# Head norms in phases, one row moved ahead on ScalarE, and first weights loaded by halves, in a fused four-branch encoder layer

## The chip, the cores and the metric

One Trainium2 chip, one of its cores. The metric is the device time of one execution in microseconds (us); lower is better.

## The reference

One layer of a bidirectional encoder over 2048 positions of width 1024, in float32. The input is RMS-normalised and projected once into 11 slots of 256 columns. Four mixers of 256 channels read these slots, each is multiplied by a SiLU gate, and one output projection of 1024 by 1024 adds the result to the input.

```python
def reference(x, mem, norm_g, w_in, w_out, ...):
    for l in range(DEPTH):
        h = rmsnorm(x, norm_g[l])
        proj = h @ w_in[l]
        a_u, a_v, a_g, b_q, b_k, b_v, b_g, c_in, c_g, d_q, d_g = jnp.split(proj, N_IN_SLOTS, axis=-1)
        y_a = chunked_spatial_gating(a_u, a_v, ...) * jax.nn.silu(a_g)
        y_b = neighbourhood_attention(b_q, b_k, b_v, ...) * jax.nn.silu(b_g)
        y_c = fourier_mixing(c_in, fn_w[l]) * jax.nn.silu(c_g)
        mem_n = rmsnorm(mem, mem_norm_g[l])
        y_d = memory_attention(d_q, mem_n, ...) * jax.nn.silu(d_g)
        x = x + jnp.concatenate([y_a, y_b, y_c, y_d], axis=-1) @ w_out[l]
```

Both attentions normalise each query and key head of 64 channels by its own RMS ("QK-norm"). That is the norm the change takes apart.

## The kernel before

**Precision and tiling.** Every operand of a large matmul is split into a high and a low part (`hi` rounded to fp32r, `lo` = raw - hi), and a product is three matmuls: hi*hi, hi*lo, lo*hi. x comes transposed, in tiles of 128 contraction rows by 512 positions (`get_x`, line 187; ScalarE makes hi on L137, VectorE makes lo on L138). Weights come two contraction steps at a time, 128 x 2 x 256, 256 KB (`get_w`, line 201): one DMA on L207, hi on ScalarE (L217), lo on GpSimd, or on VectorE for the second of two interleaved slots (`alt`) (L219). x, weights and `w_out` share five `raw` landing buffers.

**Order.** TensorE's order is written out by hand: `drive` (line 163) runs a filler (the projections) and spawned tasks (norms, transposes, attention, Fourier), and a task gives TensorE back by `yield d`, which makes it due again after d us of TensorE work. All other queues (ScalarE, VectorE, GpSimd, SP) are ordered by a list scheduler at build time: program order, moved up by `hp(offset)`. Each queue then runs strictly in its order.

**The sequence.** The sequence positions are in two halves, h = 0 and 1. For h = 0: `c_in` and `d_q` interleaved, one contraction step at a time, four groups of each (`proj`, `slot`); after 48 of these 64 groups `stats` (line 281) loads x in natural layout for the RMS (16 loads into five `nat` buffers, squares on L291, `rstd` by GpSimd on L294/L125). Then `pair_vv`, `a_u`, `pair_qk`, `a_g`, `d_g`, `b_g`, `c_g`; the same slots for h = 1; the output projection last (`out_proj`). Beside `pair_vv` run the memory keys and values (`mem_kv`, line 467; its squares are L495, each behind a load of `mem` on L494 into a `nat` buffer), the transposes of the queries (`emit_T` on L151 and L534/L535) and `bcast` (line 297).

**Norms of queries and keys.** `do_dq` (line 421) and `do_bqk` (line 431) take four PSUM banks. For each bank in turn `evac_nat` copies it to a `nat` tile scaled by `rstd` (L368, L370), and `head_norm` (line 373) squares it on ScalarE (L376), sums the heads on VectorE (L378), takes the power -1/2 on GpSimd (L124, L125) and scales in place on VectorE (L381). The task then yields 6.5 us (14 for the first `d_q`) and transposes.

**The row of norms.** `bcast` transposes `rstd` on TensorE into a PSUM tile, ScalarE copies the 8 x 128 row out (L302, at no raised priority), and two DMAs spread it over all partitions (L304, L306).

**Pipelined attention.** `pipeline` (line 546) runs scores two units ahead of transposes: while the first two score units go out, it yields `d[0]` after each (1.2 us for the memory attention, 0.3 for the other). Its two calls are the memory attention of h = 0, and everything that is left of both attentions.

Of the kernel before, what the change touches and what calls it, by code (L numbers as in the profile page):

```python
# [9 lines left out]
F32 = mybir.dt.float32  # L10
F32R = mybir.dt.float32r
AF = mybir.ActivationFunctionType
ALU = mybir.AluOpType
# [34 lines left out]
class Kern:  # L48
# [151 lines left out]

    def get_w(self, name, k, c0, alt):
        nc = self.nc
        with self.hp(8000 if k or alt else 15000 if self.wseen else 80000):
            raw = self.raw.tile([128, 2, 256], F32, name="raw")
            begin = not self.wseen and not alt
            self.wseen = True
            (nc.scalar if begin else nc.sync).dma_start(out=raw, in_=self.ins[name][k * 128:(k + 2) * 128, c0:c0 + 256].rearrange(  # L207
                "(t p) c -> p t c", t=2))
            if alt:
                w = self.att.tile([128, 2, 2, 256], F32R, name="PT", bufs=2)  # L210
                w = [w[:, 0], w[:, 1]]
            else:
                w = [self.wp.tile([128, 2, 256], F32R, name="hilo") for _ in range(2)]
            if begin:
                nc.vector.tensor_copy(out=w[0], in_=raw)
            else:
                nc.scalar.copy(out=w[0], in_=raw)  # L217
            eng = nc.vector if alt else nc.gpsimd
            eng.tensor_tensor(out=w[1], in0=raw, in1=w[0].bitcast(F32), op=ALU.subtract)  # L219
        return w  # L220

    def get_w2(self, k, ia, ib):
# [25 lines left out]
    def slot(self, h, c0, natural, ps, kstep):  # L248
        alt = bool(ps)
        if not ps:  # L250
            ps.extend(self.ps_acc.tile([128, 512], F32, name="acc") for _ in range(4))
        for k0 in range(0, 8, kstep):
            ks = range(k0, k0 + kstep)
            Xs = [self.get_x(h, k) for k in ks]
            if k0 % 2 == 0:
                wp = self.get_w("w_in", k0, c0, alt)
            for b in range(4):
                for k in ks:
                    X = Xs[k - k0]
                    wh, wl = wp[0][:, k % 2], wp[1][:, k % 2]  # L260
                    st, sp = k == 0, k == 7
                    if natural:
                        for t in (2 * b, 2 * b + 1):
                            o = ps[b][:, (t % 2) * 256:(t % 2) * 256 + 256]
                            xh, xl = X[t // 4]
                            sl = slice((t % 4) * 128, (t % 4) * 128 + 128)
                            first = st and t % 2 == 0
                            last = sp and t % 2 == 1
                            self.mm(o, xh[:, sl], wh, first, False, skip_group_check=True)
                            self.mm(o, xh[:, sl], wl, False, False, skip_group_check=True)  # L270
                            self.mm(o, xl[:, sl], wh, False, last, skip_group_check=True)
                    else:
                        cj, t = b // 2, b % 2
                        sl = slice(cj * 128, cj * 128 + 128)
                        xh, xl = X[t]
                        self.mm(ps[b], wh[:, sl], xh, st, False)
                        self.mm(ps[b], wh[:, sl], xl, False, False)
                        self.mm(ps[b], wl[:, sl], xh, False, sp)
                    yield
# [17 lines left out]
    def bcast(self, h):  # L297
        nc = self.nc
        ps = self.ps_mi.tile([8, 128], F32, name=self.nmi)
        self.tr(ps, self.rstd[h])  # L300
        row = self.sqp.tile([8, 128], F32, name="sa_o")
        nc.scalar.activation(out=row, in_=ps, func=AF.Copy, scale=0.5)  # L302
        d = self.d([8, 128], f"rs{h}")
        nc.sync.dma_start(out=d, in_=row)  # L304
        bc = self.const.tile([128, HS], F32, name="rbc")
        nc.sync.dma_start(out=bc, in_=d.rearrange("t p -> (t p)").unsqueeze(0).broadcast_to([128, HS]))  # L306
        self.rbc[h] = bc
        if h == 0:
            for cj in range(2):
                nc.gpsimd.tensor_tensor(out=self.cin[cj][:, 0:HS], in0=self.cin[cj][:, 0:HS], in1=bc, op=ALU.mult)  # L310
        yield
# [61 lines left out]
    def head_norm(self, q):  # L373
        nc = self.nc
        sq = self.sqp.tile([128, 512], F32, name="sq")
        nc.scalar.activation(out=sq, in_=q, func=AF.Square)  # L376
        ss = self.small.tile([128, 8], F32, name="hss")
        nc.vector.tensor_reduce(out=ss, in_=sq.rearrange("p (g d) -> p g d", d=HD), axis=AX.X, op=ALU.add)  # L378
        self.rsqrt(ss, ss, 1.0 / HD, 8)
        qv = q.rearrange("p (g d) -> p g d", d=HD)  # L380
        nc.vector.tensor_tensor(out=qv, in0=qv, in1=ss.unsqueeze(2).broadcast_to([128, 8, HD]), op=ALU.mult)  # L381
        return q
# [37 lines left out]

    def do_dq(self, h, ps):
        with self.hp(8000):
            qs = [self.head_norm(self.evac_nat(h, [(ps[b][:, j * 256:(j + 1) * 256], 2 * b + j) for j in range(2)]))
                  for b in range(4)]
        yield 6.5 if h else 14.0
        for b in range(4):
            self.emit_T("d", h * 4 + b, [qs[b][:, 0:256], qs[b][:, 256:512]])
            yield 3.3
        self.done.add(f"d_q{h}")

    def do_bqk(self, h, u, ps):
        with self.hp(8000):
            qs = [self.head_norm(self.evac_nat(h, [(ps[t], u * 4 + t)])) for t in range(4)]
        yield 6.5
        for b in range(2):
            for i, kind in ((1, "k"), (0, "q")):
                self.emit_T(kind, h * 4 + u * 2 + b, [qs[2 * b + j][:, i * 256:(i + 1) * 256] for j in range(2)])
                yield 3.3
        if u:
            self.done.add(f"b_qk{h}")  # L440
# [26 lines left out]
    def mem_kv(self):  # L467
        nc, I = self.nc, self.ins
        ps = [self.ps_sc.tile([128, 512], F32, name=self.nsc) for _ in range(2)]
        for k in range(8):  # L470
            with self.hp(0):
                raw = self.att.tile([128, 256], F32, name="dq", bufs=2)
                nc.sync.dma_start(out=raw, in_=I["memT"][k * 128:(k + 1) * 128, :])
                if k % 2 == 0:
# [6 lines left out]
                                               in1=m[:, 0].bitcast(F32), op0=ALU.mult, op1=ALU.subtract)  # L481
                if k % 2 == 0:
                    wt = self.att.tile([128, 2, 2, 512], F32R, name="PT", bufs=2)
                w = [wt[:, k % 2, 0], wt[:, k % 2, 1]]
# [5 lines left out]
        ss = self.c([128, 2, 2], "mss")  # L490
        for t in range(2):
            for u in range(2):
                raw = self.nat.tile([128, 512], F32, name="nat")
# [5 lines left out]
        q = self.nat.tile([128, 512], F32, name="nat")  # L499
# [8 lines left out]
            nc.vector.tensor_tensor(out=self.vm[:, t, :, HD:2 * HD], in0=v4,  # L508
                                    in1=self.vm[:, t, :, 0:HD].bitcast(F32), op=ALU.subtract)
        self.psum(True)  # L510
        self.head_norm(q)
        twice = self.att.tile([128, 512, 2], F32, name="PT", bufs=2)
        nc.vector.tensor_copy(out=twice, in_=q.unsqueeze(2).broadcast_to([128, 512, 2]))
        self.spawn(self.mem_k(twice), 20.0)
# [31 lines left out]
    def pipeline(self, items, d):  # L546
        A = 2
        units, n = [], 0
        last = {}
        it = iter(items)  # L550
        more = True
        while more or n < len(units) + A + 1:
            if n >= len(units) and more:
                try:
                    us, pv = next(it)
                    units.extend(us)
                    last[len(units) - 1] = pv
                except StopIteration:
                    more = False
            if n < len(units):  # L560
                units[n][0]()
                yield d[0]
            if 0 <= n - A < len(units):
                units[n - A][1]()
                yield d[1]
            if n - A - 1 in last:
                last.pop(n - A - 1)()
                yield d[2]
            n += 1
# [566 lines left out]
    def run(self):  # L1136
        tc = self.tc
        self.X, self.rstd, self.rbc = {}, {}, {}
        self.wseen = False
        self.t, self.seq, self.tasks, self.done = 0.0, 0, [], set()  # L1140
        self.scratch()
        self.constants()
        with tc.manual_schedule(engines={mybir.EngineType.PE}):
            with ExitStack() as es:
                P = lambda name, bufs, st=es: st.enter_context(tc.tile_pool(name=name, bufs=bufs, side="right",
                                                                            reuse_waits="tile"))
                self.nat = P("nat", 5)
                self.sqp = P("sqp", 2)
                self.att = P("att", 2)
                self.psum(False)  # L1150
                self.drive(self.main(P, es))
                self.pst.close()
# [98 lines left out]
```

## Time and profile before

| | |
|---|---|
| median of 3 runs | 872.2 us (871.57 to 875.5) |
| the profiled execution | 872.36 us, of which 870.6 is the span from its first to its last instruction |
| TensorE matmuls (PE) | 852.1 us busy, 98% of the span, 4448 matmuls |
| TensorE weight loads (PEld) | 82% |
| VectorE (DVE), ScalarE (ACT), GpSimd (POOL) | 58%, 47%, 38% |
| DMA | 177.9 MB, 204 GB/s on average |

A busy PE is matmuls in flight, so the 2% that is not busy is time in which TensorE waited for someone. "Granted clock" is the share of 2.4 GHz that the throttle gave; 0.5 is 1.2 GHz.

### The profile page before, as it was taken

Reading aid. Unit: us, or ns where it says so; the run is one execution under the profiler, and the core shown is the slowest. Engines: PE = TensorE matmul, PEld = TensorE weight load, DVE = VectorE, ACT = ScalarE, POOL = GpSimd, SP = SyncE. Lnnn points to the kernel's source line nnn. Section 1 sums busy time; section 2 is a strip of 40 time slices with the busy share of each in tenths; the row PEclk is TensorE's granted clock in tenths of the full one; section 3 lists DMA queues with packets and bytes.
Section 4 is the critical chain, followed back from the end, with each engine's and each line's share of the span. In section 5 each row is a group of like instructions: output and inputs, shape, how many; then the busy total and the mean of one; then the engine's idle time right before and its main releaser. Section 6 shows DMA issues by size and latency. Waiting matters only on the chain.

```text
span 870.6 us, 13653 instructions
## 1 busy us (share of the span) xinstructions
PE 852.1 (98%) x4448; PEld 713.6 (82%) x4448; DVE 502.6 (58%) x1064; ACT 407.1 (47%) x930; POOL 327.2 (38%) x368
## 2 busy tenths in 40 slices
PE   8999999999999999999999999999999999999998
PEld 7987788888788878887789888888878788888886
DVE  5356565587532557775454866676788777851111
ACT  5674353466632533544324655666765455521110
POOL 1136331155232122552232734434554433235550
PEclk9999999999999999999999999999999999999999
DMA  8967653346762562569669897864598987556661
GB/s 274 323 202 231 191 141 109 117 118 176 227 192 96 187 215 84 142 169 278 210 194 306 265 299 246 263 213 142 175 311 280 320 243 221 174 168 195 205 204 68
DMA packets 147463, 177.88 MB, mean 204 GB/s; under 512 B 29232, under 2 KB 105152, under 8 KB 147392
## 3 DMA queue, kind: packets, MB, share of 16 engines
q1 hardware_dynamic: 145104, 170.33, 62.6%
q0 software_dynamic: 1728, 6.29, 2.5%
q8 instruction: 35, 0.57, 0.3%
q10 hardware_dynamic: 560, 0.40, 0.2%
q14 instruction: 36, 0.29, 0.1%
HBM read 132.92 MB, written 44.05 MB: 203 GB/s over the span
## 4 chain that ended last, share of the span: by engine, by line
PE 78%; DMA 9%; DVE 6%; ACT 3%; issue 2%; POOL 2%; SPq 0%; ACTq 0%; DVEq 0%; POOLq 0%
PE acc L147 60%; PE w L147 8%; PE w L151 4%; PE sc L147 3%; DMA bt<-in_bias 2%; PE mi L147 2%; DMA nat<-in_mem 1%; DMA QD<-st 1%; DMA raw<-in_w_out 1%; DVE PT L535 1%; POOL hss L125 1%; DVE P L916 1%; DMA raw<-in_w_in 1%; DVE hilo L990 1%; DMA nat<-in_x 0%
## 5 line engine op out<-in xcount | busy, mean ns | idle before, releaser
L147 PE MATMUL acc<-hilo 128*128 128x512 f32 (+1 forms) x2880 | 710.5, 390 | 7.6 <-DVE nat L460 1.9
L147 PEld LDWEIGHTS acc<-hilo 128*128 128x128 f32 x2880 | 510.0, 189 | 100.1 <-issue 2.9
L219 POOL TENSOR_TENSOR hilo<-raw,hilo 128x512 fp32r<-128x512 f32 x52 | 68.5, 1319 | 171.2 <-ACT hilo L217 141.5
L231 POOL TENSOR_TENSOR hilo<-raw,hilo 128x512 fp32r<-128x512 f32 x32 | 43.3, 1352 | 114.4 <-ACT hilo L229 93.8
L983 POOL TENSOR_TENSOR nat<-nat 128x256 f32<-128x256 f32 x48 | 36.7, 764 | 93.4 <-DMA nat<-O 61.9
L229 ACT CAST hilo<-raw 128x512 fp32r<-128x512 f32 x64 | 39.7, 621 | 65.9 <-PE acc L147 54.9
L918 ACT ACTIVATE P<-P,smx 128x288 f32<-128x288 f32 (+1 forms) x64 | 39.9, 623 | 54.1 <-DVE smx L916 54.0
L535 DVE TENSOR_TENSOR PT<-w,PT 128x512 fp32r<-128x512 f32 (+2 forms) x96 | 61.2, 637 | 5.6 <-ACT PT L534 5.6
L1027 DVE TENSOR_TENSOR st<-acc,st 128x512 f32<-128x512 f32 (+1 forms) x33 | 21.6, 671 | 70.2 <-PE acc L147 69.9
L989 ACT CAST hilo<-nat 128x256 fp32r<-128x256 f32 x64 | 25.7, 406 | 76.3 <-PE acc L147 57.2
L534 ACT CAST PT<-w 128x512 fp32r<-128x512 f32 (+2 forms) x96 | 52.1, 543 | 18.6 <-PE w L151 18.0
L151 PE MATMUL w<-ident,P 128*128 128x128 f32 (+1 forms) x352 | 54.2, 273 | 1.0 <-DVE smx L916 1.0
L151 PEld LDWEIGHTS w<-ident,P 128*128 128x128 f32 (+1 forms) x352 | 43.0, 135 | 14.6 <-DVE smx L916 1.9
L217 ACT CAST hilo<-raw 128x512 fp32r<-128x512 f32 x51 | 31.3, 618 | 47.9 <-PE acc L147 35.4
L125 POOL TENSOR_TENSOR hss<-hss,mhalf 128x8 f32<-128x8 f32 x25 | 42.7, 1712 | 1.5
L916 DVE CUSTOM_DVE_ANT_0 P<-w,bt 128x288 f32<-128x288 f32 (+1 forms) x64 | 35.6, 556 | 13.2 <-DMA bt<-in_bias 10.3
L231 DVE TENSOR_TENSOR hilo<-raw,hilo 128x512 fp32r<-128x512 f32 x32 | 22.0, 689 | 31.0 <-ACT hilo L229 25.5
L607 ACT ACTIVATE P<-w,smx 128x256 f32<-128x256 f32 x64 | 29.7, 469 | 20.5 <-DVE smx L603 20.2
L958 POOL TENSOR_TENSOR ob<-tmp 64x128 f32<-64x128 f32 x64 | 30.1, 489 | 21.8 <-DVE tmp L954 20.6
L345 DVE TENSOR_TENSOR st<-acc,rbc 128x512 f32<-128x512 f32 x32 | 22.0, 686 | 26.4 <-PE acc L147 23.5
L138 DVE SCALAR_TENSOR_TENSOR hilo<-raw,gcol,hilo 128x512 fp32r<-128x512 f32 x32 | 26.2, 829 | 17.5 <-ACT hilo L137 16.6
L921 DVE TENSOR_SCALAR P<-P,smx 128x288 f32<-128x288 f32 (+1 forms) x64 | 34.0, 531 | 1.8
(170 smaller groups left out, 1062.7 us busy)
## 6 DMA issues: line engine op xcount, KB each, us to landing
raw<-in_w_in SPq DMA_DIRECT2D x119, 256.0 KB, 3.1
raw<-in_xT SPq DMA_DIRECT2D x32, 256.0 KB, 3.8
nat<-in_x SPq DMA_DIRECT2D x32, 256.0 KB, 5.3
G<-st SPq DMA_DIRECT2D x32, 256.0 KB, 3.4
nat<-G SPq DMA_DIRECT2D x64, 128.0 KB, 2.8
st<-in_x SPq DMA_DIRECT2D x32, 256.0 KB, 4.9
out_y<-st SPq DMA_DIRECT2D x31, 256.0 KB, 3.3
tab<-in_dft_s POOLq DMA_DIRECT2D x12, 512.0 KB, 5.2
```

Of the source, the lines that this page charges most:

```text
L125: nc.gpsimd.tensor_tensor(out=out, in0=out, in1=self.mhalf[:, :n], op=ALU.pow)
L147: self.nc.tensor.matmul(out=out, lhsT=lhsT, rhs=rhs, start=start, stop=stop, **k)
L151: self.nc.tensor.transpose(out=out, in_=in_, identity=self.ident)
L219: eng.tensor_tensor(out=w[1], in0=raw, in1=w[0].bitcast(F32), op=ALU.subtract)
L229: nc.scalar.copy(out=w[0], in_=raw)
L231: eng.tensor_tensor(out=w[1], in0=raw, in1=w[0].bitcast(F32), op=ALU.subtract)
L534: self.nc.scalar.copy(out=hi, in_=src)
L535: (eng or self.nc.vector).tensor_tensor(out=lo, in0=src, in1=hi.bitcast(F32), op=ALU.subtract)
L916: nc.vector.tensor_tensor_reduce(out=P[:, :n], in0=sc[:, :n], in1=bt[:, :n], op0=ALU.add, op1=ALU.min, scale=-1.0, scalar=3e38, accum_out= ...
L918: nc.scalar.activation(out=P[:, :n], in_=P[:, :n], func=AF.Exp, bias=sm[:, 1:2], scale=-1.0, accum_out=sm[:, 2:3])
L921: nc.vector.tensor_scalar(out=P[:, :n], in0=P[:, :n], scalar1=sm[:, 3:4], scalar2=None, op0=ALU.mult)
L983: mul.tensor_tensor(out=g, in0=o, in1=g, op=ALU.mult)
```

## The change

- `get_w`: the first load of each of the first two slots (`c_in` and `d_q`, k = 0) fetches only its first contraction step (128 KB), on ScalarE's DMA queue, with the highest priority; its hi and lo are made for that half alone (`c_in`: VectorE and GpSimd; `d_q`: ScalarE and VectorE). The other half is loaded on SP's queue when the slot reaches k = 1, and split by GpSimd (`c_in`) or VectorE (`d_q`) with a copy and a subtraction. First weights of later slots lose their offset of 15000 and get 8000 like all others.
- `bcast`: L302 gets the offset 9000.
- `head_norm` stops before the scaling, which becomes `scale_norm`. `do_dq` and `do_bqk` evacuate all four banks, take all four norms, yield 2.5 us, scale all four, and yield 4.5 us (12 for the first `d_q`).
- `pipeline`: 1.5 us more yield after each of the first two score units.

```diff
@@ -200,23 +200,34 @@
 
     def get_w(self, name, k, c0, alt):
         nc = self.nc
-        with self.hp(8000 if k or alt else 15000 if self.wseen else 80000):
+        with self.hp(8000 if k or self.wseen > 1 else 80000):
             raw = self.raw.tile([128, 2, 256], F32, name="raw")
-            begin = not self.wseen and not alt
-            self.wseen = True
-            (nc.scalar if begin else nc.sync).dma_start(out=raw, in_=self.ins[name][k * 128:(k + 2) * 128, c0:c0 + 256].rearrange(
-                "(t p) c -> p t c", t=2))
+            begin = k == 0 and self.wseen < 2
+            self.wseen += 1
+            src = self.ins[name][k * 128:(k + 2) * 128, c0:c0 + 256].rearrange("(t p) c -> p t c", t=2)
+            if begin:
+                nc.scalar.dma_start(out=raw[:, 0], in_=src[:, 0])
+            else:
+                nc.sync.dma_start(out=raw, in_=src)
             if alt:
                 w = self.att.tile([128, 2, 2, 256], F32R, name="PT", bufs=2)
                 w = [w[:, 0], w[:, 1]]
             else:
                 w = [self.wp.tile([128, 2, 256], F32R, name="hilo") for _ in range(2)]
+            eng = nc.vector if alt else nc.gpsimd
             if begin:
-                nc.vector.tensor_copy(out=w[0], in_=raw)
+                (nc.scalar.copy if alt else nc.vector.tensor_copy)(out=w[0][:, 0], in_=raw[:, 0])
+                eng.tensor_tensor(out=w[1][:, 0], in0=raw[:, 0], in1=w[0][:, 0].bitcast(F32), op=ALU.subtract)
             else:
                 nc.scalar.copy(out=w[0], in_=raw)
-            eng = nc.vector if alt else nc.gpsimd
-            eng.tensor_tensor(out=w[1], in0=raw, in1=w[0].bitcast(F32), op=ALU.subtract)
+                eng.tensor_tensor(out=w[1], in0=raw, in1=w[0].bitcast(F32), op=ALU.subtract)
+        if begin:
+            def rest():
+                with self.hp(8000):
+                    nc.sync.dma_start(out=raw[:, 1], in_=src[:, 1])
+                    eng.tensor_copy(out=w[0][:, 1], in_=raw[:, 1])
+                    eng.tensor_tensor(out=w[1][:, 1], in0=raw[:, 1], in1=w[0][:, 1].bitcast(F32), op=ALU.subtract)
+            self.rest[alt] = rest
         return w
 
     def get_w2(self, k, ia, ib):
@@ -254,6 +265,8 @@
             Xs = [self.get_x(h, k) for k in ks]
             if k0 % 2 == 0:
                 wp = self.get_w("w_in", k0, c0, alt)
+            elif k0 == 1 and alt in self.rest:
+                self.rest.pop(alt)()
             for b in range(4):
                 for k in ks:
                     X = Xs[k - k0]
@@ -299,7 +312,8 @@
         ps = self.ps_mi.tile([8, 128], F32, name=self.nmi)
         self.tr(ps, self.rstd[h])
         row = self.sqp.tile([8, 128], F32, name="sa_o")
-        nc.scalar.activation(out=row, in_=ps, func=AF.Copy, scale=0.5)
+        with self.hp(9000):
+            nc.scalar.activation(out=row, in_=ps, func=AF.Copy, scale=0.5)
         d = self.d([8, 128], f"rs{h}")
         nc.sync.dma_start(out=d, in_=row)
         bc = self.const.tile([128, HS], F32, name="rbc")
@@ -377,6 +391,10 @@
         ss = self.small.tile([128, 8], F32, name="hss")
         nc.vector.tensor_reduce(out=ss, in_=sq.rearrange("p (g d) -> p g d", d=HD), axis=AX.X, op=ALU.add)
         self.rsqrt(ss, ss, 1.0 / HD, 8)
+        return ss
+
+    def scale_norm(self, q, ss):
+        nc = self.nc
         qv = q.rearrange("p (g d) -> p g d", d=HD)
         nc.vector.tensor_tensor(out=qv, in0=qv, in1=ss.unsqueeze(2).broadcast_to([128, 8, HD]), op=ALU.mult)
         return q
@@ -420,9 +438,14 @@
 
     def do_dq(self, h, ps):
         with self.hp(8000):
-            qs = [self.head_norm(self.evac_nat(h, [(ps[b][:, j * 256:(j + 1) * 256], 2 * b + j) for j in range(2)]))
+            qs = [self.evac_nat(h, [(ps[b][:, j * 256:(j + 1) * 256], 2 * b + j) for j in range(2)])
                   for b in range(4)]
-        yield 6.5 if h else 14.0
+            ss = [self.head_norm(q) for q in qs]
+        yield 2.5
+        with self.hp(8000):
+            for q, s in zip(qs, ss):
+                self.scale_norm(q, s)
+        yield 4.5 if h else 12.0
         for b in range(4):
             self.emit_T("d", h * 4 + b, [qs[b][:, 0:256], qs[b][:, 256:512]])
             yield 3.3
@@ -430,8 +453,13 @@
 
     def do_bqk(self, h, u, ps):
         with self.hp(8000):
-            qs = [self.head_norm(self.evac_nat(h, [(ps[t], u * 4 + t)])) for t in range(4)]
-        yield 6.5
+            qs = [self.evac_nat(h, [(ps[t], u * 4 + t)]) for t in range(4)]
+            ss = [self.head_norm(q) for q in qs]
+        yield 2.5
+        with self.hp(8000):
+            for q, s in zip(qs, ss):
+                self.scale_norm(q, s)
+        yield 4.5
         for b in range(2):
             for i, kind in ((1, "k"), (0, "q")):
                 self.emit_T(kind, h * 4 + u * 2 + b, [qs[2 * b + j][:, i * 256:(i + 1) * 256] for j in range(2)])
@@ -508,7 +536,7 @@
             nc.vector.tensor_tensor(out=self.vm[:, t, :, HD:2 * HD], in0=v4,
                                     in1=self.vm[:, t, :, 0:HD].bitcast(F32), op=ALU.subtract)
         self.psum(True)
-        self.head_norm(q)
+        self.scale_norm(q, self.head_norm(q))
         twice = self.att.tile([128, 512, 2], F32, name="PT", bufs=2)
         nc.vector.tensor_copy(out=twice, in_=q.unsqueeze(2).broadcast_to([128, 512, 2]))
         self.spawn(self.mem_k(twice), 20.0)
@@ -559,7 +587,7 @@
                     more = False
             if n < len(units):
                 units[n][0]()
-                yield d[0]
+                yield d[0] + (1.5 if n < A else 0)
             if 0 <= n - A < len(units):
                 units[n - A][1]()
                 yield d[1]
@@ -1136,7 +1164,7 @@
     def run(self):
         tc = self.tc
         self.X, self.rstd, self.rbc = {}, {}, {}
-        self.wseen = False
+        self.wseen, self.rest = 0, {}
         self.t, self.seq, self.tasks, self.done = 0.0, 0, [], set()
         self.scratch()
         self.constants()
```

## Rows read from the trace of the kernel before

**Rows 1.** The page, part 1: busy time of TensorE and its share of the span.

```profile
PE 852.1 (98%) x4448; PEld 713.6 (82%) x4448; DVE 502.6 (58%) x1064; ACT 407.1 (47%) x930; POOL 327.2 (38%) x368
```

**Rows 2.** Busy time by stretch: us, then each engine (instructions), granted clock, DMA share, GB/s.

```profile
5.00:8.41 3.41, 1.10 (x6) 0.46 (x5) 2.76 (x4) 2.06 (x3) 1.71 (x1) 1.00 0.80 253
8.41:11.83 3.42, 3.42 (x13) 3.00 (x14) 2.74 (x8) 1.67 (x3) 0.00 (x0) 0.50 0.87 271
...
72.95:75.13 2.18, 0.40 (x2) 0.00 (x0) 0.85 (x2) 1.93 (x6) 0.83 (x2) 1.00 0.86 254
...
93.75:97.16 3.41, 1.69 (x7) 0.94 (x6) 2.42 (x5) 1.36 (x3) 1.87 (x2) 1.00 0.64 182
97.16:100.57 3.41, 3.41 (x9) 2.65 (x9) 2.43 (x7) 0.62 (x1) 1.80 (x3) 0.50 0.60 160
100.57:768.00 667.43, 660.14 (x3522) 552.65 (x3522) 431.89 (x938) 335.69 (x776) 248.42 (x272) 1.00 0.66 203
```

**Rows 3.** Timeline 0 to 9 us: start, duration, instruction, [idle before <- releaser].

```profile
0.72 0.40 ACTq L94 DMA_DIRECT2D gcol<-in_gcol  x1
...
1.16 0.48 ACTq L207 DMA_DIRECT2D raw<-in_w_in  x1
...
4.13 0.72 ACT L137 ACTIVATE hilo<-raw,gcol 128x512 fp32r<-128x512 f32 x1 [0.97 <-DMA gcol<-in_gcol]
...
6.03 0.43 DVE L215 CAST hilo<-raw 128x512 fp32r<-128x512 f32 x1 [0.39 <-DMA raw<-in_w_in]
...
6.54 1.71 POOL L219 TENSOR_TENSOR hilo<-raw,hilo 128x512 fp32r<-128x512 f32 x1 [5.24 <-DVE hilo L215]
...
8.30 0.71 PE L147 MATMUL acc<-hilo 128*128 128x512 f32 x1 [1.00 <-POOL hilo L219]
```

**Rows 4.** DMA queues, 3.4 to 4.5 us: ScalarE's queue (q10), packets, MB, share.

```profile
q10 hardware_dynamic: 105, 0.11, 41.5%
```

**Rows 5.** The page, costliest groups: busy us, mean ns of one, idle before.

```profile
L219 POOL TENSOR_TENSOR hilo<-raw,hilo 128x512 fp32r<-128x512 f32 x52 | 68.5, 1319 | 171.2 <-ACT hilo L217 141.5
...
L983 POOL TENSOR_TENSOR nat<-nat 128x256 f32<-128x256 f32 x48 | 36.7, 764 | 93.4 <-DMA nat<-O 61.9
...
L217 ACT CAST hilo<-raw 128x512 fp32r<-128x512 f32 x51 | 31.3, 618 | 47.9 <-PE acc L147 35.4
```

**Rows 6.** Timeline 46 to 76 us: TensorE's transposes that restart after the wait.

```profile
75.13 0.66 PE L151 MATMUL mi<-ident,nat 128*128 128x128 f32 x4 [1.78 <-ACT sa_o L302]
```

**Rows 7.** Timeline 46 to 76 us: the end of ScalarE's queue before that row.

```profile
73.20 0.63 ACT L495 ACTIVATE nat<-nat 128x512 f32<-128x512 f32 x1 [1.99 <-DMA nat<-in_mem]
...
73.83 0.56 ACT L534 CAST st<-mi 128x512 fp32r<-128x512 f32 x1
...
74.30 0.62 ACT L229 CAST hilo<-raw 128x512 fp32r<-128x512 f32 x1
...
74.82 0.26 ACT L302 ACTIVATE sa_o<-mi 8x128 f32<-8x128 f32 x1
```

**Rows 8.** The same timeline: the last load and the last square of the statistics.

```profile
47.89 0.33 SPq L290 DMA_DIRECT2D nat<-in_x  x1
...
52.76 0.59 ACT L324 COPY cin<-acc 128x512 f32<-128x512 f32 x1 [0.83 <-PE acc L147]
...
53.25 0.63 ACT L291 ACTIVATE nat<-nat 128x512 f32<-128x512 f32 x1
...
54.00 0.33 SPq L494 DMA_DIRECT2D nat<-in_mem  x1
```

**Rows 9.** The page, DMA issues: count, KB each, median us from issue to landing.

```profile
raw<-in_xT SPq DMA_DIRECT2D x32, 256.0 KB, 3.8
nat<-in_x SPq DMA_DIRECT2D x32, 256.0 KB, 5.3
```

**Rows 10.** Timeline 211 to 223 us: second norm of the tightest batch, its first transposes.

```profile
214.31 1.77 DVE L381 TENSOR_TENSOR nat<-nat,hss 128x512 f32<-128x512 f32 x1 [0.20 <-POOL hss L125]
...
218.08 0.60 PE L151 MATMUL w<-ident,nat 128*128 128x128 f32 x4
```

**Rows 11.** Line 219 as a source: who waited for it (us, times).

```profile
  PE acc L147: 1.0, 1
```

## The prediction

> **What bounds the kernel now.** I read the page first: TensorE is busy 852.1 of 870.6 us [rows 1], so a change off TensorE can only give back some of the 18.5 us in which it waits, and what it loses to a lower clock. Then the busy time by stretch [rows 2]. From 100.57 to 768 us TensorE is idle 7.3 us in all, in many small waits. The costly places lie early, and this change aims at two of them. At the start, TensorE works 1.10 us of the 3.41 before 8.41 us, and the next 3.42 us run at a granted clock of 0.50, which is 1.2 GHz: 13 matmuls that would take half of that at 2.4 GHz, so 1.71 us are lost. At 72.95 us it stands nearly still until 75.13. (A third place, 93.75 to 97.16 and 3.41 us of half clock behind it, isn't touched.) After that I took the timeline of the two places and followed each wait back.
>
> At the start [rows 3] the third matmul waits until 8.30 us for GpSimd's low part of the first weights, which took 1.71 us after VectorE's cast at 6.03, which waited for the 256 KB of weights. At 72.95 the transposes of the second query block restart at 75.13, released by L302 [rows 6]. But ScalarE's queue shows what L302 itself stood behind [rows 7]: a square of `mem` (L495) that waited 1.99 us for its load, then the evacuation L534 of the first block (priority 8000), then a weight cast L229 (8000), then L302 at 74.82.
>
> **The change part by part.** The sum is made against the profiled execution, 872.36 us (span 870.6 and 1.8 around it); the median of 872.2 is 0.16 below it.
>
> First weights by halves. In 3.4 to 4.5 us ScalarE's DMA queue, which then carries little but these weights, moved 0.11 MB [rows 4]; a half is 0.13 MB, so it is in at about 4.7, and I estimate 5.0 with its signal, against 6.03. The bounds: not before 4.13, where `gcol`, ahead in the same queue, released ScalarE; not after 5.5, which is 128 KB less at the 253 GB/s of that stretch [rows 2, 3]. The half cast takes about 0.25 (half of 0.43), GpSimd's subtraction on 128x256 takes 0.76 (the same shape on L983 [rows 5]), so the low part stands at 6.05 and the third matmul starts at 6.1 instead of 8.30. `d_q`'s half is second in the same queue and lands where the whole first load landed, at 6.0; copied by ScalarE (0.31, half of L217) and subtracted it is ready near 6.8. For that and for the second x tile I allow 0.9 us of waits. The 13 matmuls then take 1.71 us at full clock, so by 6.1 + 1.71 + 0.9 = 8.7 TensorE has done what it had done at 11.83: **3.1 us earlier**, 1.4 from the loads and 1.7 from the clock. Bounds: 0.9 (landing at 5.5, clock low as before) to 3.9 (landing at 4.3, no waits).
>
> The Trainium skill ("DMA: Bandwidth & Descriptors", "Issuing engines are not separate DMA queues") says that transfers issued by different engines interleave on the same 16 engines and that a second issuing engine saves only issue time. By it the half gains by its bytes alone, the start would give 2.6 instead of 3.1, and rival 1 below 867.8. The trace agrees that the engines are shared: this queue had 41.5% of their time in that stretch [rows 4], and the 3.1 goes by what it moved.
>
> The second halves. Two more loads on SP and, on GpSimd, a copy and a subtraction of 128x256. The trace has no GpSimd copy; it lies between nothing and the 0.76 of a subtraction with one input more, and I take 0.76, since it is the same shape and engine. The 1.5 us lie in GpSimd's idle time (5.24 us idle before its first subtraction [rows 3]), and are due when k = 1 begins, after the 36 matmuls of k = 0: at 1.71/13 = 0.13 each some 4.7 us behind 6.1. So they cost nothing; uncovered they would cost 1.5 once. VectorE's half of `d_q` is the same with 0.7.
>
> The row ahead on ScalarE. Offset 9000 lets L302 pass what is ready at the same time. L534 belongs to transposes that TensorE does before the row's own, and it already has 8000; yet it came out behind L495, which has no offset. So when the queue was laid out L495 was placed before L534 was ready, and L302, ready later still, can't pass L495 by priority. What it surely passes is L229: 74.30 instead of 74.82, **0.5 us**.
>
> So the gate stays, and the earlier start meets it. L495's load comes from a chain: the last square of the statistics (53.25, behind a copy L324 that waits for TensorE) frees the `nat` buffer in which the first `mem` load goes out at 54.00 [rows 8], and four loads and squares follow one another through it. The copy moves forward with TensorE, but the square needs its load, issued at 47.89. With the median of such loads, 5.3, it lands at 53.2 and the chain doesn't move; with the 3.8 of equal loads of `xT` it lands at 51.7 and the chain moves 1.5 [rows 9]. No row says which, so I take **1.0**, between the two, and keep 0 to 1.5. The row's time is then 75.13 - 0.5 - 1.0 = 73.6.
>
> Norms in phases. No operation is added; the scaling is emitted 2.5 us of TensorE work later and the transposes 0.5 later. The 0.5 us of projection matmuls thus comes ahead of the gate: **0.5** more is done when it opens. For the other batches I cost it at nothing: in the tightest one the second scaling ends at 216.1 and its transposes start at 218.1 [rows 10], 2.0 us of cover, 2.5 with the later yield. If the scaling slid by the full 2.5 us there, the wait would be about zero; by a further GpSimd power, some 2 us in one batch.
>
> Later first weights (8000 instead of 15000) and 1.5 us more yield after the first two score units of two pipelines: nothing. After the start no matmul waits for GpSimd's low weights (one wait of 1.0 us, the one above) [rows 11], ScalarE's cast L217 waits for TensorE to free buffers rather than the other way (35.4 us [rows 5]), and a yield only lets other matmuls go first. Should a slot's first weights lose their cover, rival 3 has the price.
>
> Sum: at the gate TensorE is 0.5 + 1.0 + 0.5 = 2.0 us ahead, less than the 3.1 it brought, and it keeps that to the end: 872.36 - 2.0 = 870.4, or **870.2** beside the median.
>
> **The rivals.** (1) The row gets past L495, because the new order of the norms or the earlier start shifts what is ready when the queue is laid out. Then nothing holds TensorE at 72.95: 3.1 + 1.8 idle = 4.9 us, **867.3**. For it: only one queue position decides. Against it: L534 had a priority too and didn't pass.
>
> (2) The gate costs the clock too. TensorE reaches it at 72.95 - 3.1 + 0.5 = 70.35 and stands up to 3.25 us. In 93.75 to 97.16 it was idle 1.72 us and the clock fell to 1.2 GHz for the next 3.41; at 72.95 it was idle 1.78 and the clock stayed [rows 2]. A fall costs 1.7 and leaves **871.9**. The Trainium skill ("TensorE: Matmul & The Clock Gate", "Part 1: The HAM clock gate") says that the monitor runs free of the program, so that the same idle time may or may not lower the clock; the trace agrees, by those two stretches.
>
> (3) Slower: the first weights of the ten later slots, no longer with 15000, are cast behind the evacuations at each slot's start, and TensorE waits there. It decides from the point where these weights come later than the last ones run out. Price: a cast and a subtraction, 0.62 + 1.32 = 1.94 us [rows 5], ten times 19.4, less the 2.0: **889.6**, or half of it if half the slots are hit. Against it stands that now none waits [rows 11].
>
> (4) It does less than it says: L302 passes nothing, the chain doesn't move, and only the later yield counts: 0.5 us, **871.7**.
>
> **How the numbers follow.** Forecast 0.40, rival 1 0.28, rival 2 0.16, rival 3 0.07, rival 4 0.09. About 0.5% (4.4 us) is what a measurement of this kernel can tell from no change. Rival 1 lies across that line, so three quarters of it count as faster, and 0.06 of the forecast: 0.27. Slower is rival 3 and a tail of rival 2: 0.09. The rest, 0.64, is within. The range goes from 865.5 (rival 1 with the upper bound of the start, 3.9, and 1 us of other small waits gone) to 873.8 (rival 2 with 1.9 us of new small waits, as the queues are all laid out anew); rival 3 is left out.
>
> **What would show it.** Right: the third matmul near 6.1 us, no stretch of 0.50 before 12 us; TensorE still idle near 70 to 74 us, released by L302 behind L495; matmuls unchanged in number. Wrong: no idle time there (rival 1); a 0.50 stretch behind it (rival 2); several waits of TensorE for L217 or L219 after 100 us (rival 3); or a new wait for scalings (L381), which would be the moved norms.

## The result, and the profile after

The changed kernel took **886.19 us** (median of 4 runs: 882.61, 882.65, 889.74, 891.68), the kernel before 871.94 beside it: a ratio of **1.0146 [1.0113, 1.0179]**. The prediction was 870.2 us, and its range ended at 873.8. The time is 12.4 us beyond that end, on the side to which 0.09 was given. The profiled execution took 891.68 us (span 889.7), one of the two long ones among the four; a second profile of the same kernel (e5 below) has a span of 883.4.

TensorE did the same matmuls with little more busy time, so the loss is waiting, as the page's part 1 shows (compare [rows 1]):

```profile
PE 856.3 (96%) x4448; PEld 715.6 (80%) x4448; DVE 499.5 (56%) x1066; ACT 407.0 (46%) x930; POOL 328.1 (37%) x370
```

Busy time by stretch, columns as in [rows 2], says where:

```profile
5.00:8.41 3.41, 2.22 (x8) 0.89 (x7) 2.86 (x5) 1.75 (x3) 2.40 (x3) 1.00 0.66 216
8.41:11.83 3.42, 3.42 (x24) 3.15 (x25) 3.19 (x9) 1.76 (x3) 0.36 (x1) 1.00 0.67 215
53.00:60.00 7.00, 4.29 (x12) 2.41 (x11) 1.58 (x3) 5.72 (x15) 2.25 (x3) 0.77 0.23 85
56.78:63.60 6.82, 5.95 (x15) 4.16 (x14) 4.42 (x9) 5.68 (x15) 4.30 (x4) 0.50 0.28 82
70.00:76.00 6.00, 6.00 (x30) 4.91 (x29) 5.09 (x9) 3.47 (x8) 5.71 (x5) 1.00 0.43 106
...
100.57:111.40 10.83, 1.07 (x9) 0.65 (x9) 0.16 (x1) 4.31 (x12) 0.89 (x2) 0.68 0.52 152
111.40:114.80 3.40, 3.40 (x19) 2.69 (x16) 2.23 (x5) 1.99 (x5) 0.95 (x2) 0.50 0.00 0
```

In this execution the clock stays at 1.00 up to 11.83 us, as predicted, though the third matmul starts at about 7.15 us and not at 6.1. The wait near 73 us is gone: TensorE is busy all through 70 to 76. New are a slow stretch at 53 to 63.6 us and, costliest, a wait near 101 us in which TensorE works 1.07 of 10.83 us, with 3.40 us of work at 1.2 GHz behind it (the 0.68 of the row says that the clock fell while TensorE still waited). The view of waits, TensorE alone, names what ended them:

```profile
PE w L147 <- ACT sq L533: 9.8, 1, 9.8
PE w L147 <- DVE PT L563: 7.2, 8, 2.5
PE acc L147 <- ACT cin L338: 2.7, 3, 1.1
...
PE acc L147 <- DVE nat L488: 1.3, 2, 1.1
```

L533 is `mem_kv` emptying its PSUM tile (the first of its two): the shared PSUM pool that `mem_kv` opens next reuses that memory, and the first matmuls that want it are those of the spatial gating (`w<-wsT,nat`). The chain of waits from 96 to 112 us, followed back from TensorE's restart at 110.87, shows why it comes so late (start, duration, what):

```profile
95.26 4.20 DMA V<-nat
...
99.48 0.03 SPq L522
...
99.54 3.15 DMA nat<-in_mem
...
103.75 0.73 ACT nat L523 x2
...
104.50 3.39 DMA nat<-in_mem
...
109.98 0.47 ACT nat L530
110.45 0.38 ACT sq L533
...
110.87 1.33 PE w L147 x9
```

The loads of `mem` (L522, before L494) waited for a store of *values* to leave a `nat` buffer, and the four loads and squares went one after another through what came free. Before, the same four loads were issued between 54.0 [rows 8] and 70.3 us; now between 98.4 and 104.5. No priority of the squares and no operation on them was changed.

To say what each place is worth, I counted the columns that the matmuls of both traces had streamed and compared the times at equal work (after minus before): -2.0 us from 16 to 52 us, +6.3 from 52 to 60, -2.1 from 72 to 76 (the old wait gone), -2.3 from 92 to 100, **+11.5 from 100 to 104** (9.8 of wait and 1.7 of clock), and +8.3 in several places from 395 us to the end; with small changes between, +19.3 in all. Such a count of one execution is called the ledger below.

**Theory A**: the half microsecond by which the first `d_q`'s yields grew (2.5 + 12.0 for 14.0) does it. TensorE's hand-written order, before and after, from the timeline of TensorE; `sc<-PT,P` x6 is one of `mem_kv`'s eight contraction steps, and the L151 lines are the first query transposes:

```profile
67.09 1.55 PE L147 MATMUL sc<-PT,P 128*128 128x512 f32 x6
68.48 0.86 PE L147 MATMUL acc<-hilo 128*128 128x512 f32 x3
69.17 0.60 PE L151 MATMUL mi<-ident,nat 128*128 128x128 f32 x4
...
85.61 1.55 PE L147 MATMUL sc<-PT,P 128*128 128x512 f32 x6
```

```profile
71.40 1.55 PE L147 MATMUL sc<-PT,P 128*128 128x512 f32 x6
72.79 1.55 PE L147 MATMUL acc<-hilo 128*128 128x512 f32 x6
74.18 0.60 PE L151 MATMUL mi<-ident,nat 128*128 128x128 f32 x4
...
91.99 1.55 PE L147 MATMUL sc<-PT,P 128*128 128x512 f32 x6
```

Six projection matmuls stand before the transposes where three stood, and every later turn of the tasks falls elsewhere. `mem_kv`'s last step used to come ahead of the first values (85.61 against their first evacuation, L456, at 88.6); now it comes behind them (91.99 against 87.6). Only after that step does the task ask for the `nat` buffers of its squares, so it now asks behind the values and gets its buffers when the values are done with them.

### The profile page after: what moved, and what is told of

Read it like the earlier page. It is cut to its first block, busy times and chain, and to the rows that moved or that the text cites. A ratio compares the mean times of both kernels' runs of the same rounds, so it can differ in the third digit from the quotient of the medians.

```text
span 889.7 us, 13669 instructions
## 1 busy us (share of the span) xinstructions
PE 856.3 (96%) x4448; PEld 715.6 (80%) x4448; DVE 499.5 (56%) x1066; ACT 407.0 (46%) x930; POOL 328.1 (37%) x370
## 4 chain that ended last, share of the span: by engine, by line
PE 62%; DMA 17%; DVE 7%; ACT 5%; issue 3%; POOL 3%; SPq 1%; ACTq 0%; DVEq 0%; POOLq 0%
PE acc L147 49%; PE w L147 6%; DMA nat<-in_x 3%; DMA bt<-in_bias 3%; DMA raw<-in_xT 3%; PE w L151 3%; PE sc L147 3%; DMA raw<-in_w_in 1%; DMA G<-st 1%; POOL hss L125 1%; DMA QD<-st 1%; PE mi L147 1%; DMA nat<-G 1%; DMA O<-z 1%; ACT nat L304 1%
## 5 line engine op out<-in xcount | busy, mean ns | idle before, releaser
L223 POOL TENSOR_TENSOR hilo<-raw,hilo 128x512 fp32r<-128x512 f32 x51 | 67.2, 1320 | 158.5 <-ACT hilo L222 138.8
L242 POOL TENSOR_TENSOR hilo<-raw,hilo 128x512 fp32r<-128x512 f32 x32 | 42.4, 1325 | 129.9 <-ACT hilo L240 115.1
L1055 DVE TENSOR_TENSOR st<-acc,st 128x512 f32<-128x512 f32 (+1 forms) x33 | 21.5, 667 | 70.5 <-PE acc L147 70.4
L151 PE MATMUL w<-ident,P 128*128 128x128 f32 (+1 forms) x352 | 54.2, 273 | 0.5 <-DVE tmp L982 0.5
L151 PEld LDWEIGHTS w<-ident,P 128*128 128x128 f32 (+1 forms) x352 | 42.9, 135 | 14.2 <-DVE tmp L982 1.4
L944 DVE CUSTOM_DVE_ANT_0 P<-w,bt 128x288 f32<-128x288 f32 (+1 forms) x64 | 35.7, 557 | 12.9 <-DMA bt<-in_bias 10.2
L147 PEld LDWEIGHTS w<-PT,vt 96*128 96x128 f32 (+1 forms) x160 | 27.6, 191 | 14.9 <-DVE PT L563 10.0
L147 PE MATMUL w<-PT,vt 96*128 96x256 f32 (+3 forms) x160 | 32.8, 336 | 6.8 <-DVE PT L563 6.8
L949 DVE TENSOR_SCALAR P<-P,smx 128x288 f32<-128x288 f32 (+1 forms) x64 | 35.9, 562 | 1.7
```

The source lines that it names most:

```text
L147: self.nc.tensor.matmul(out=out, lhsT=lhsT, rhs=rhs, start=start, stop=stop, **k)
L151: self.nc.tensor.transpose(out=out, in_=in_, identity=self.ident)
L944: nc.vector.tensor_tensor_reduce(out=P[:, :n], in0=sc[:, :n], in1=bt[:, :n], op0=ALU.add, op1=ALU.min, scale=-1.0, scalar=3e38, accum_out= ...
L949: nc.vector.tensor_scalar(out=P[:, :n], in0=P[:, :n], scalar1=sm[:, 3:4], scalar2=None, op0=ALU.mult)
```

## The experiments

The texts on record name their theories by letters, each with what it says. Ratios are against the kernel before, run beside each group (medians 874.56 us for e1 to e4, 875.36 for e5 to e8, 874.60 for e9 to e12, 875.76 for e13). Line numbers are each kernel's own.

**e1: the half microsecond alone, in the kernel before.**

```diff
-        yield 6.5 if h else 14.0
+        yield 6.5 if h else 14.5
```

> The kernel before with one number changed: the first query task yields 14.5 us instead of 14.0, nothing else. Theory A (the half microsecond does the damage: it puts the first transposes later, so that the task of the memory keys ends only after the first value pair has ended, asks for its nat buffers behind the values, and holds a PSUM tile for which TensorE then waits): the memory squares come after the values' evacuations on ScalarE, TensorE waits about 10 us once near 100 us, the wait for the row at 73 us is gone; by the stretches of the changed kernel -2.1, -2.3 and +11.5 us, so 879 us (877 to 882). Theory B (taking the norms in phases does it, because scalings come later and buffers are held longer): nothing is taken in phases here, so 872 us.

880.89 us, **1.0070 [1.0048, 1.0093]**. Its view of waits, TensorE alone, and its loads of `mem` as a source:

```profile
PE w L147 <- ACT sq L505: 10.2, 1, 10.2
```

```profile
L494 SPq DMA_DIRECT2D nat<-in_mem x4: 340/344/458, 93.8 to 99.8; - x4
```

One constant makes the whole wait, with nothing else of the change, and the time is where theory A put it (877 to 882). The ledger has the same three marks: -2.1 from 72 to 76 us, -2.9 from 92 to 100, +12.3 from 100 to 104.

**e2: the changed kernel with the old totals** (2.5 + 11.5, and 2.5 + 4.0 for the others).

```diff
-        yield 4.5 if h else 12.0
+        yield 4.0 if h else 11.5
...
-        yield 4.5
+        yield 4.0
```

> The changed kernel with all its edits, but with the total yields of the kernel before (2.5 + 11.5 and 2.5 + 4.0 instead of 2.5 + 12 and 2.5 + 4.5). Theory A: the memory squares are back before the values, the 10 us wait is gone and the old waits near 73 and 95 us return; 7 us less than the changed kernel, 876 to 880 us in the median. Theory B: still 886 us.

877.67 us, **1.0035 [1.0018, 1.0052]**; the wait on the squares is gone. What is left is small and in many places, the largest 4.9 us behind the values' L488.

**e5 and e6: the changed kernel again, and with buffers of their own for the squares** of `mem`; both keep the longer yields.

```diff
-                raw = self.nat.tile([128, 512], F32, name="nat")
+                raw = self.sqp.tile([128, 512], F32, name="sq")
```

> The changed kernel once more, unchanged, beside the next three on one chip and with more runs. 1.2 to 1.7% above the kernel before; the 10 us wait near 100 us is there again, since the queues' orders are fixed; the loss near 55 us is there again, with or without a fall of the clock.

> The changed kernel with the four squares of the memory rows loaded into the two buffers of the squares (sq) instead of the five nat buffers; yields as in the change. Theory A (the half microsecond hurts because the squares queue for nat buffers behind the values): with buffers of their own they run early again though the yields stay, the 10 us wait goes, the one near 95 us goes too; 10 to 13 us less than the changed kernel run beside it. Rival F (the late emission itself puts them behind, whatever buffers they use): same as the changed kernel.

e5: 885.34 us, 1.0133 [1.0102, 1.0163], with 10.2 us of the same wait. e6: 874.46 us, **1.0006 [0.9988, 1.0024]**. The views of waits, TensorE alone, of e5:

```profile
PE w L147 <- ACT sq L533: 10.2, 1, 10.2
PE w L147 <- DVE PT L563: 4.8, 7, 1.1
```

and of e6:

```profile
PE w L147 <- DVE PT L563: 5.8, 5, 2.5
PE acc L147 <- DVE nat L488: 2.8, 1, 2.8
```

Of the 1.33%, 1.27 (11 us) hang on which buffers those four squares use. In e6 the last step of `mem_kv` still comes behind the first value (88.05 us against 83.7), yet the loads of `mem` go out from 63.8 to 68.9: with buffers of their own the order does no harm. e5 has no slow stretch at 53 us, against its expectation (no matmul there waits for `cin`): that +6.3 belongs to the profiled execution of after, where loads of x for the statistics came late, ScalarE's squares stood waiting for them, and the copies L338 of `c_in` stood behind the squares. That it makes the two long runs among the four is not shown.

**e13: the order alone.** Yields and shared buffers stay; `mem_kv` begins 1 us earlier.

```diff
-        self.spawn(self.mem_kv(), 5, 0)
+        self.spawn(self.mem_kv(), 4, 0)
```

> The changed kernel with the memory task spawned to begin after 4 us of TensorE work instead of 5; the yield of 14.5 us in all and the shared nat buffers stay. Theory A (the order in which the two tasks ask for buffers decides): the four squares of mem stand ahead of the values again, so the wait of some 10 us near 101 us that ends in a square of mem is gone, and the time is 8 to 12 us below the changed kernel, 874 to 878. Rival (the later yield itself costs the time, or the kind of buffer does, whatever the order): the wait or one of its size stays near 100 us and the time is 883 to 888.

877.55 us, **1.0028 [1.0012, 1.0045]**, the 10 us wait gone. Its loads of `mem`, as a source:

```profile
L522 SPq DMA_DIRECT2D nat<-in_mem x4: 327/328/419, 58.2 to 70.5; - x4
```

Five kernels with shared buffers now stand side by side (us; the first value is L456 or L484); the loss goes with the order, not with the yield:

| | yields | last step of `mem_kv` | first value evacuated | loads of `mem` issued | 10 us wait |
|---|---|---|---|---|---|
| before | 14.0 | 85.61 | 88.6 | 54.0 to 70.3 | no |
| e2 | 14.0 | 84.19 | 87.2 | 57.3 to 70.5 | no |
| e13 | 14.5 | 85.46 | 89.6 | 58.2 to 70.5 | no |
| e1 | 14.5 | 88.06 | 83.7 | 93.8 to 99.8 | 10.2 |
| after | 14.5 | 91.99 | 87.6 | 98.4 to 104.5 | 9.8 |

**e3, e4, e10 and e12: one part each, in the kernel before**: the edit of `get_w` (with its second halves and the lower offset of later slots); the 1.5 us in `pipeline`; the norms in phases at the old totals of 14.0 and 6.5; the offset of the row.

```diff
-        with self.hp(8000 if k or alt else 15000 if self.wseen else 80000):
+        with self.hp(8000 if k or self.wseen > 1 else 80000):
...
-                yield d[0]
+                yield d[0] + (1.5 if n < A else 0)
...
+        yield 2.5
...
+        yield 4.0 if h else 11.5
...
+        with self.hp(9000):
+            nc.scalar.activation(out=row, in_=ps, func=AF.Copy, scale=0.5)
```

> The kernel before with the edit of the first weights alone. Theory C (the earlier start runs into the statistics: ScalarE's copies of c_in stand behind squares that wait for loads of x, and TensorE waits there with a fall of its clock): -2.0 us at the start, +6.3 near 55 us, of which the later gate near 73 us may take back up to 2: 874 to 877 us. Theory D (the start's gain is kept, the loss near 55 us comes from the norms in phases): 869 to 870 us.

> The kernel before with the 1.5 us more yield after the first two score units alone. Theory E (these yields move the attention against the output projection, and cause the 7.8 us that the changed kernel loses between 400 and 750 us): 876 to 880 us. Theory A holds them harmless: 871 to 873 us.

> The kernel before with the norms in phases and the totals of the yields kept at 14.0 and 6.5. Theory A (phases are harmless as such, the half microsecond is not): within 2 us of the kernel before. Theory B (phases cost): 5 us or more above it; the waits then are of transposes for scalings.

> The kernel before with the offset of the row alone. By the prediction it passes only one weight cast: 0.5 us less at the wait near 73 us, which stays; 0 to 0.5 us in all. If it passes the memory square too, the wait is gone: 2 us less.

e3: 878.36 us, **1.0040 [1.0022, 1.0058]**: the loads that were to bring 3.1 us lose some 3.5. Both theories missed; C's loss at the statistics is there, but small, and most is lost elsewhere. Busy time by stretch of e3:

```profile
5.00:8.15 3.15, 1.76 (x6) 0.67 (x4) 2.49 (x4) 1.85 (x3) 2.03 (x3) 1.00 0.65 209
8.15:11.56 3.41, 3.22 (x12) 2.93 (x13) 2.83 (x10) 1.45 (x2) 0.72 (x1) 0.50 0.65 212
...
96.89:103.72 6.83, 5.25 (x12) 3.95 (x13) 4.85 (x11) 1.97 (x4) 3.66 (x4) 0.50 0.61 168
```

Here the clock fell at the start in spite of the earlier weights, so the ledger's gain at 48 us is 0.4. By 60 us that is lost, and 1.0 more, behind a copy of `c_in` (1.0 us of wait). The waits for values are 3.7 us instead of 1.9, and the half clock behind them lasts 6.83 us instead of 3.41 [rows 2]: some 4 us between 92 and 96. Why the values came later is not shown.

e4: 875.79 us, 1.0006 [0.9987, 1.0026], nothing. e10: 876.19 us, 1.0018 [0.9995, 1.0040], nothing that this measurement can tell. e12: 875.04 us, 1.0005 [0.9984, 1.0025]. ScalarE in the timeline of e12, to hold against [rows 7] (its lines are one higher from L303 on):

```profile
73.79 0.63 ACT L496 ACTIVATE nat<-nat 128x512 f32<-128x512 f32 x1 [1.95 <-DMA nat<-in_mem]
...
74.42 0.56 ACT L535 CAST st<-mi 128x512 fp32r<-128x512 f32 x1
74.88 0.62 ACT L229 CAST hilo<-raw 128x512 fp32r<-128x512 f32 x1
75.40 0.26 ACT L303 ACTIVATE sa_o<-mi 8x128 f32<-8x128 f32 x1
```

The row still stands last, behind the square and even behind L229, which the prediction had it pass. TensorE waits 1.6 us for it instead of 1.8.

The five parts alone come to 0.70 + 0.40 + 0.18 + 0.06 + 0.05 = 1.39%, beside 1.33% and 1.46% measured for the whole. It fits, but each term is uncertain by some 0.2% and they share buffers and queues, so it is no proof that they add.

**e7, e8, e9 and e11: what is left once the squares have their own buffers.** All have e6's edit. e7 is e6 with the copies of `c_in` on VectorE (`nc.vector.tensor_copy` in place of `nc.scalar.copy`); e8 is the kernel before with e6's edit alone; e9 is e8 with the new first weights and the copies on VectorE; e11 is e6 without the 1.5 us in `pipeline`.

> The kernel of e6 with the four copies of c_in out of PSUM on VectorE instead of ScalarE, so that they no longer stand behind squares that wait for x. Theory C (that order on ScalarE gives the start's gain back and more): no wait of TensorE near 55 us, 3 to 6 us less than e6, and less than the kernel before by 2 to 4 us. Rival G (TensorE then waits just behind, at the first memory matmul, for d_q's PSUM tiles, which need the same statistics): within 1.5 us of e6.

> The kernel before with the memory squares in the sq buffers, nothing else. If nat buffers were what held the values near 95 us (their evacuation waits for a value's store to free one), that wait of 3.7 us with its fall of the clock goes: 2 to 4 us less than the kernel before. If it was the stores themselves or ScalarE's order, no difference.

> The kernel before with the edit of the first weights, the memory squares in buffers of their own and the c_in copies on VectorE; norms, row and yields as before. Theory A and C together: the start's 2 us (0 to 0.5 in executions whose clock falls there) and what the buffers give (0.2% in e8) are kept, nothing waits at 55 or 100 us: 2 to 4 us less than the kernel before. Rival H (what is won early is lost between 230 and 750 us, whatever wins it): within 1 us of the kernel before.

> The kernel of e6 without the 1.5 us more yield of the score units. Theory E' (this yield, with the phases, makes the 4 to 5 us that e5 and e6 lose between 470 and 750 us): 3 to 5 us less than e6, so below the kernel before by as much. Theory I (these losses come from the layout of the queues, which every edit shuffles): within 2 us of e6, the losses at other places.

| | median us | ratio to before |
|---|---|---|
| e7 | 874.88 | 0.9996 [0.9973, 1.0020] |
| e8 | 872.89 | **0.9978 [0.9959, 0.9997]** |
| e9 | 873.71 | 0.9988 [0.9966, 1.0010] |
| e11 | 873.92 | 0.9993 [0.9972, 1.0015] |

e7 missed: no matmul waits for `cin` any more, and nothing is gained that can be measured. e8 is the only version faster than both kernels: 0.2%, at the edge of its interval. The size is the expected one, the reason is not: TensorE still waits for values (2.3 us instead of 1.9), but with the squares done earlier the wait for the row near 73 us is gone (2.0 us in the ledger), and the granted clock is 1.00 from 94 to 112 us. e9, which was to gain 2 to 4 us, shows nothing that the first weights add to it. The ledger of e6 ends at +4.9 us, nearly all from after 470 us; that of e11 at -1.2 with none there. Their medians differ by 0.5 us only, so that these late losses come from the added yields is not shown; they stay open, and so do those of after (+8.3 from 395 us, +4.5 in e5).

## Why the prediction was wrong

**The step that failed** is "Norms in phases": "The 0.5 us of projection matmuls thus comes ahead of the gate: **0.5** more is done when it opens." The half microsecond was costed as a gain of 0.5 us; by itself it costs 6.1 to 6.3 (e1: 0.70%). I looked at what comes ahead of the gate and at the cover of the scalings, and not at what the later yield moves behind it: another task's last step, and with it who asks first for shared buffers. The trace of before had what was needed: the last step of `mem_kv` at 85.61 us and the first value at 88.6 stood 3 us apart, and both tasks use `nat`.

**A second term failed**, the "**3.1 us earlier**" of the start, of which the sum kept 1.0 through the chain of squares: alone, the first weights cost 0.40% (e3). In e9, with own buffers for the squares and the copies on VectorE, they cost nothing that can be measured (0.9988 beside e8's 0.9978), so this loss too seems to hang on the buffers or the copies; which of them is not shown.

**Rival 3** had the sign and nearly the size (889.6) by another mechanism: L223, the later slots' low weights, has nobody who waited for it. That part of the prediction held.

**Start.** "I estimate 5.0" for the landing of the half was too early. Timeline of after, 5 to 9 us:

```profile
5.55 0.29 DVE L219 CAST hilo<-raw 128x256 fp32r<-128x256 f32 x1 [4.66 <-DMA raw<-in_w_in]
...
5.93 1.17 POOL L220 TENSOR_TENSOR hilo<-raw,hilo 128x256 fp32r<-128x256 f32 x1 [4.63 <-DVE hilo L219]
...
7.05 0.86 POOL L228 CAST hilo<-raw 128x256 fp32r<-128x256 f32 x1
...
7.98 0.78 POOL L229 TENSOR_TENSOR hilo<-raw,hilo 128x256 fp32r<-128x256 f32 x1
```

The half lands at the upper bound, 5.5, and GpSimd's first subtraction takes 1.17 us instead of 0.76; the low part stands at 7.1 instead of 6.05, still 1.2 us before the 8.30 of [rows 3]. The Trainium skill ("DMA: Bandwidth & Descriptors", "Issuing engines are not separate DMA queues") has queues share the engines, by which the half gains by its bytes alone; the cast at 5.55 agrees. The bound of 3.9 doesn't come out of its terms either (3.1 + 0.7 for the landing + 0.9 of waits is 4.7); that would have lowered the low end of the range, not the end that was passed.

The 1.7 us from the clock was counted as sure and is not. The ledger's gain at 48 us was 2.0 and 2.1 us in after and e2, where matmuls ran at full speed from 8.3 us on, but 0.8 in the second profile of after (e5) and 0.4, 0.5 and 0.2 in e3, e6 and e13, which had a stretch at half clock.

**The chain of squares** was to move 1.0 us earlier with the start. Where the squares kept their place (e2, e13), their first load went out at 57.3 and 58.2 us, later than the 54.0 of [rows 8], and about a microsecond behind the end of the statistics' last square, which began at 55.35 and 56.29 instead of 53.25: it stands in a row of squares that wait for loads of x, and these did not come earlier with TensorE. The start's gain did not even reach the gate: the ledgers lose 2.2 us from 52 to 60 us in e2 and 2.9 in e13 (6.3 in after, 1.4 in e3), where TensorE waits for copies of `c_in` behind those squares, and nothing there in e1, e4, e8, e10 and e12, which have the old first weights.

**The row and the gate.** "What it surely passes is L229" is wrong (e12), worth under 1 us. That the gate stays held in e10 and e12, where TensorE waits 2.6 and 1.6 us for the row. In after it opened, but for a reason that rival 1 did not have: the last square of `mem` ran at 108.0 us instead of 73.2, so the row came at 75.29 us right behind its transpose. Rival 1's gain (2.1 us in the ledger) was paid for with 11.5.

**Clock.** Rival 2 put the fall at the gate. In e10 and e12, where TensorE waits there, the clock stayed at 1.00 from 68 to 94 us. In after it fell in the waits at 53 to 63.6 us (0.50 from 56.78) and during the 9.8 us wait; behind that, 111.40 to 114.80 cost the 1.7 us that the prediction gives for one such stretch.

**Nothing, as said:** the scalings (no one waited for L399), the second halves on GpSimd (0.86 + 0.78 us, covered), and the yields in `pipeline` (e4).

## What to carry to other kernels

Where tasks are woven by yields and share a pool of buffers, a yield is not a local delay: list, for each task that runs beside the one you change, its last step and the first request of its neighbour, and see whether the change can swap them (here 3 us of distance, moved by half a microsecond of yield, made a wait of 10 us and cost 6). A long wait whose releaser is an evacuation should be followed back to the load in front of it and to who held that load's buffer. A gain at the start of a kernel counts only if what the next wait hangs on moves with it (here loads of x, which did not).

## What the runs showed of the hardware that was not expected

The clock near the start is not set by the program alone. After and e5 are the same kernel: in after, three matmuls of 512 columns from 8.93 us took 0.86 us, at 2.4 GHz; in e5, three from 9.53 took 1.41 and three from 11.50 took 0.86, so e5 ran at half clock until shortly before 11 us. The Trainium skill ("TensorE: Matmul & The Clock Gate", "Part 1: The HAM clock gate") says that the monitor runs free of the program; these two executions agree. In after TensorE had worked 2.22 us of the 3.41 before 8.41 us; in e3, with the same first loads, 1.76 of 3.15, and it ran at 1.2 GHz for the next 3.41 us. Where the clock's records begin late, the view of stretches prints 1.00 without them: for e8 it gives 1.00 from 8 to 12 us, but six matmuls of 256 columns took 1.48 us from 9.05 and 0.88 from 13.65.

GpSimd's 128x256 operations at the start took 1.17, 0.86 (a copy) and 0.78 us: here a copy with one input cost no less than a subtraction with two, where the prediction had put it at 0.76 at most, and the first subtraction took half as much again. The same three times stand in e3 and e5; why the first is longer is not shown, for VectorE was at work beside all three.
